# Turning residual columns and rotated heads by DMA instead of TensorE, loading weights five chunks ahead, and taking the heads' roots on GpSimd, in a two-layer hybrid encoder

## The chip, the cores and the metric

The kernel runs on one core of a Trainium2 chip. The metric is the device time of one execution in microseconds (us); the median of several runs is given. A core has TensorE (PE, with weight loads shown apart as PEld), VectorE (DVE), ScalarE (ACT), GpSimd (POOL) and SyncE (SP, which here issues transfers only). Each engine works through its own queue in order; engines wait for each other by semaphores.

## The reference, cut to what matters

The input is 256 tokens of width 2048, in float32. Two layers, each "norm, input projection, two kinds of attention with a SiLU gate, output projection, add", and a last norm.

```
def rms_norm(x, g):
    y = x * rsqrt(mean(x * x, axis=-1, keepdims=True) + EPS)
    return y * g

h = x
for layer in range(2):
    y = rms_norm(h, norm_g[layer])
    h = h + (even_layer(y, ...) if layer == 0 else odd_layer(y, ...))
return rms_norm(h, final_g)

# even: A = dilated attention (8 heads), B = neighbourhood attention (8 heads)
# odd:  C = windowed attention with a sink (8 heads, 2 for k and v)
#       D = dense attention (8 heads of q, 2 of k and v), q and k normed and rotated:
q = axial_rope(rms_norm(q, gq)); k = axial_rope(rms_norm(k, gk))
logits = einsum('bqhgd,bshd->bhgqs', q, k) * scale
p = softmax(logits); o = einsum('bhgqs,bshd->bqhgd', p, v)
# all: mix = concat of o * silu(gate); layer output = mix @ w_out
```

A head is 128 wide. What matters here are three places: the residual h behind the even layer must be turned (features onto partitions) to be the odd layer's input; each head of D needs one root per token for q and for k; the normed and rotated heads must be turned, too, before the logits.

## The kernel before, in words

**Numbers.** Every float32 factor is split in two, a rounded high part and the rest (`split`: ACT makes the high part, DVE subtracts). Products are sums of three matmuls, high by high, high by rest, rest by high (`mm3`, L102 to L104; `by_feature` does the same in two kinds of matmul, L267 and L271).

**Weights.** Every weight matrix is cut in chunks of 128 x 1024 (512 KB), in one list, `plan`, in the order of use. Class `Weights` (L55 on) loads a chunk to `wraw` (pool `wp`, 5 buffers, on SP, L65), ACT casts it to `whi` (L69) and DVE subtracts to `wlo` (L70), 3 buffers of each. `weights()` hands out the next chunk and prepares chunks so that two are ready beyond it (AHEAD = 2). One chunk is what TensorE works on between two calls of `step()`.

**Steps.** `step()` runs behind each chunk and lets three lists go on by a piece: `evac` (accumulators to SBUF), `post` (norm and rotation of D's heads, `normed_rope`, and the start of D's attentions) and `bg` (attentions, `attend`, written as generators). That sets where instructions are issued; the scheduler then sets the final order on each engine, and instructions marked with `keep_in_program_order` (the function `pinned` for transfers on SP) keep theirs.

**Stages.** Even layer: four groups of heads, each values by tokens (`ps_t`) and q, k, gates by features (`ps_f`), with the attentions of the group before alongside. Then the even output projection `project_out("even", next_input)`: four column blocks n of 512, eight chunks each; when block n is complete, `add_h` adds it to the residual `h[n]` and `next_input(n)` turns it: 8 transposes by TensorE to `ps_ht` (L660), split with the norm's gain into `xh`, `xl`. Then the odd layer: pass t = 0 by tokens (k and v of D), pass 1 (q pairs 0 and 1 of D), gates of pairs 0 and 1 by features, pass 2 (q pairs 2 and 3), gates 2 and 3, then branch C by features, the odd output projection and the end (`finish`, final norm and output).

**A head pair of D.** `heads_by_token` scales the accumulators into `rq` and sums squares into `dss` on ACT. `normed_rope` takes the root of four columns (`rsqrt`, on DVE: `rs_x` L159, `rs_y` L161, then three times `rs_t`, `rs_t`, `rs_z`, L165 to L168, the last into `drr`), multiplies `rq` by it (L351), rotates into `ru`, `rw` (L358, L362, L365), transposes `ru` by TensorE to `ps_tr` (L372) and splits into `qh`, `ql` (or `kh`, `kl`). There are five such sets: k and q0 to q3.

**Transposes by DMA that are there already.** In `attend` the probabilities are turned without TensorE: POOL copies the 16-bit halves of the words apart (`ph`, L463), two DMA transposes on SP turn them (`pa`, L87), POOL puts the halves together (`pt`, L474), then they are split (L482, L483).

**POOL** does those two copies, the bias tables of B (L403) and a copy of two sink values per head of C (L427).

Of the kernel before, what the change touches and what calls it, by code (L numbers as in the profile page):

```python
# [9 lines left out]
F32 = mybir.dt.float32  # L10
F32R = mybir.dt.float32r
BF16 = mybir.dt.bfloat16
I32 = mybir.dt.int32
# [5 lines left out]
P = 128  # L19
# [12 lines left out]
AHEAD = 2  # L32
RPB_R, RPB_C = 15, 31
# [3 lines left out]
def encoder(ctx, tc, a, out):  # L37
# [4 lines left out]
    wp = pool("wp", 5)  # L42
# [11 lines left out]
    class Weights:  # L54


        def __init__(self, src, hi=None, lo=None, x=None):
            raw = wp.tile([P, 1024], F32, tag="wraw", name="wraw")
            self.hi = hi or hp.tile([P, 1024], F32R, tag="whi", name="whi")
            self.lo = lo or hp.tile([P, 1024], F32R, tag="wlo", name="wlo")  # L60
            cuts = KK if x in (0, 1) else 1
            cols = [slice(i * 1024 // cuts, (i + 1) * 1024 // cuts) for i in range(cuts)]
            for i, c in enumerate(cols):
                load = nc.sync.dma_start if x is None else pinned
                load(raw[:, c], src[:, c])  # L65
                if x is not None and i == 0:
                    pinned(xraw[x], a["xt"][x].rearrange("p (k t) -> p k t", k=KK))
            for i, c in enumerate(cols):
                nc.scalar.copy(self.hi[:, c], raw[:, c])  # L69
                nc.vector.tensor_sub(self.lo[:, c], raw[:, c], self.hi[:, c].bitcast(F32))  # L70
                if x is not None:
                    for m in (i,) if cuts > 1 else range(KK):
                        k = x * KK + m
                        split(xh[k], xl[k], xraw[x][:, m, :], gcol[:, k : k + 1])

    plan, ready = [], []

    def weights(ahead=AHEAD):

        while plan and len(ready) <= ahead:  # L80
            src, x = plan.pop(0)
            ready.append(Weights(src, x=x))
        return ready.pop(0)
# [5 lines left out]
    def split(hi, lo, src, scale=None):  # L89

        if scale is None:
            nc.scalar.copy(hi, src)
            nc.vector.tensor_sub(lo, src, hi.bitcast(F32))
        else:
            nc.scalar.mul(hi, src, scale)  # L95
            nc.vector.scalar_tensor_tensor(
                out=lo, in0=src, scalar=scale, in1=hi.bitcast(F32), op0=ALU.mult, op1=ALU.subtract
            )
# [102 lines left out]


# [13 lines left out]
    def step():  # L216

        advance(evac)
        advance(post)
        attention()  # L220

# [14 lines left out]
    def drain():  # L236
        while evac or post or bg:
            step()

# [105 lines left out]
    def normed_rope(tag, q, ss, g, scale, give):  # L345

        rr = sm.tile([P, 4], F32, tag="drr", name="drr")
        rsqrt(rr, ss, 4, 1.0 / HD)
# [17 lines left out]
        yield  # L366
        yield
        yield from room(tag)
        tr = ps_at.tile([P, 2, S], F32, tag="at", name="ps_tr")
        for t in range(2):  # L370
            for hh in range(2):
                nc.tensor.transpose(tr[:, hh, t * P : (t + 1) * P], u[:, t, hh, :], ident)  # L372
        dst = pair(tag)
        split(*dst, tr, scale)
        give(dst)
        yield

# [28 lines left out]
    def attend(idx, q, kv, silu, frees, bias=None, sink=None, shared=False):  # L406
# [110 lines left out]
        nc.vector.tensor_mul(m, o, silu)  # L517
# [33 lines left out]
    def out_plan(kind):  # L551
        plan.extend((a["w_out_" + kind][n][pr], None) for n, pr in out_order(kind))
# [7 lines left out]
    for u in range(4):  # L560
        for pr, kind in even_order(u):
            if kind == "v":
                plan.extend((a["even_t"][u][j], None if u else j) for j in range(8))
            else:
                plan.extend((a["even_f"][2 * u + pr]["qkg".index(kind)][j], None) for j in range(4))
    out_plan("even")
    for t, fs in ((0, ()), (1, (10, 11)), (2, (12, 13))):
        plan.extend((a["odd_t"][t][j], None) for j in range(8))
        plan.extend((a["odd_f"][f][j], None) for f in fs for j in range(4))
    plan.extend((a["odd_f"][f][j], None) for f in (0, 1, 2, 6, 3, 7, 4, 8, 5, 9) for j in range(4))  # L570
# [82 lines left out]

    def next_input(n):

        for c in range(2):
# [17 lines left out]

    project_out("even", next_input)
# [22 lines left out]
    def evict_heads(st, which, acc):  # L698

        for i, key in enumerate(which):  # L700
            if key is not None:
# [3 lines left out]
                post.append(normed_rope("k" if key == "k" else "q", q, ss, g, scale, give))  # L705
            yield

    def when_ready(i, st, s):
        attend_odd(1, i, st, s)
        yield  # L710

    def evict_odd(branch, kind, i, acc, st):
# [6 lines left out]
        else:  # L719
            s = gate(acc, rhalf)  # L720
            if branch:
                post.append(when_ready(i, st, s))
            else:
                attend_odd(branch, i, st, s)
# [21 lines left out]
    def beside(n, i):  # L746
# [5 lines left out]
        if n == 2 and i % 2:  # L752
            j = i // 2
            room = X[j].rearrange("p k c t -> p (k c t)")
            final.append(Weights(a["w_out_odd"][NN - 1][late[j]], room[:, :1024], room[:, 1024:]))
# [42 lines left out]
    def finish(n, t, r, cols=full, scalar=False):  # L798
# [7 lines left out]
        queue = nc.scalar if scalar and t else nc.sync  # L806
        pin(queue.dma_start(out[t * P : (t + 1) * P, n * 512 + cols.start : n * 512 + cols.stop], y))
# [17 lines left out]
    finish(0, 1, r, halves[0])  # L825
    finish(1, 1, r, scalar=True)
    finish(0, 1, r, halves[1])
    finish(2, 1, r, scalar=True)
    finish(3, 1, r, halves[0])
    finish(3, 1, r, halves[1])  # L830
# [85 lines left out]
```

## Time and profile before

| what | value |
|---|---|
| time, median of 3 runs | 820.77 us (820.68 to 821.61) |
| profiled execution | 820.54 us, of which span 818.8 us |
| granted TensorE clock, mean | 0.996 |
| PE busy | 808.6 us, 99% of the span, 4317 instructions |
| DVE busy | 576.1 us, 70%, 856 instructions |
| ACT busy | 447.3 us, 55%, 712 instructions |
| POOL busy | 110.6 us, 14%, 88 instructions |
| HBM read | 155.64 MB; 194 GB/s over the span |

The profile is of one execution. A row of the timeline gives start, duration, engine, line, operation, output<-input, shape and count. A row of groups gives count, busy time and mean duration of one in ns, then the idle time of the engine just before and what ended most of it. A row of windows gives the window and for each engine the busy us and, in brackets, the instructions: PE, PEld, DVE, ACT, POOL, then the granted clock, the DMA share and GB/s. A matmul's duration is longer than the distance to the next one because they are pipelined: the distance of starts is what it costs.

### The profile page before, as it was taken

Reading aid. Unit: us, or ns where it says so; the run is one execution under the profiler, and the core shown is the slowest. Engines: PE = TensorE matmul, PEld = TensorE weight load, DVE = VectorE, ACT = ScalarE, POOL = GpSimd, SP = SyncE. Lnnn points to the kernel's source line nnn. Section 1 sums busy time; section 2 is a strip of 40 time slices with the busy share of each in tenths; the row PEclk is TensorE's granted clock in tenths of the full one; section 3 lists DMA queues with packets and bytes.
Section 4 is the critical chain, followed back from the end, with each engine's and each line's share of the span. In section 5 each row is a group of like instructions: output and inputs, shape, how many; then the busy total and the mean of one; then the engine's idle time right before and its main releaser. Section 6 shows DMA issues by size and latency. Waiting matters only on the chain.

```text
span 818.8 us, 11775 instructions
## 1 busy us (share of the span) xinstructions
PE 808.6 (99%) x4317; PEld 695.1 (85%) x4317; DVE 576.1 (70%) x856; ACT 447.3 (55%) x712; POOL 110.6 (14%) x88
## 2 busy tenths in 40 slices
PE   9999999999999999999999999999999999999995
PEld 7888888888888888888888888888899888888884
DVE  6677675677857886587655577685987777775763
ACT  7745454554545554455445544657666665664651
POOL 0002020021302140050200000002112222221000
PEclk9999999999999999999999999999999999999998
DMA  8956765575755766565654555556577775777532
GB/s 336 354 210 209 271 213 177 208 213 168 233 182 171 241 173 220 203 194 197 213 177 172 186 186 172 200 192 198 161 183 226 224 222 184 227 197 225 209 126 104
DMA packets 90682, 166.91 MB, mean 204 GB/s; under 512 B 48960, under 2 KB 50112, under 8 KB 90560
## 3 DMA queue, kind: packets, MB, share of 16 engines
q1 hardware_dynamic: 90192, 165.61, 62.5%
q8 instruction: 34, 0.56, 0.3%
q10 hardware_dynamic: 432, 0.54, 0.2%
q14 instruction: 24, 0.20, 0.1%
HBM read 155.64 MB, written 3.05 MB: 194 GB/s over the span
## 4 chain that ended last, share of the span: by engine, by line
PE 98%; DMA 0%; ACT 0%; DVE 0%; issue 0%; ACTq 0%; DVEq 0%
PE ps_f L267 34%; PE ps_f L271 17%; PE ps_t L102 14%; PE ps_t L103 14%; PE ps_t L104 14%; PE ps_s L103 1%; PE ps_s L104 1%; PE ps_s L102 1%; PE ps_out L103 1%; PE ps_out L102 1%; PE ps_out L104 1%; PE ps_ht L660 0%; DMA wraw<-in_even_t 0%; PE ps_tr L372 0%; ACT h L803 0%; ACT whi L69 0%
## 5 line engine op out<-in xcount | busy, mean ns | idle before, releaser
L70 DVE TENSOR_TENSOR wlo<-wraw,whi 128x1024 fp32r<-128x1024 f32 (+1 forms) x270 | 344.4, 1276 | 187.8 <-ACT whi L69 187.3
L69 ACT CAST whi<-wraw 128x1024 fp32r<-128x1024 f32 (+1 forms) x270 | 281.9, 1044 | 300.9 <-PE ps_t L104 130.7
L267 PE MATMUL ps_f<-x,whi 128*128 128x512 f32 x1184 | 372.3, 396 | 0.0
L271 PEld LDWEIGHTS ps_f<-x,wlo 128*128 128x128 f32 x1184 | 222.4, 188 | 52.9 <-DVE wlo L70 0.7
L271 PE MATMUL ps_f<-x,wlo 128*128 128x256 f32 x1184 | 233.0, 278 | 0.0
L267 PEld LDWEIGHTS ps_f<-x,whi 128*128 128x128 f32 x1184 | 180.9, 189 | 0.5
L102 PE MATMUL ps_t<-whi,x 128*128 128x512 f32 (+1 forms) x256 | 96.8, 381 | 0.3 <-ACT x L95 0.3
L103 PE MATMUL ps_t<-wlo,x 128*128 128x512 f32 (+1 forms) x256 | 96.4, 379 | 0.0
L104 PE MATMUL ps_t<-whi,x 128*128 128x512 f32 (+1 forms) x256 | 96.1, 377 | 0.0
L463 POOL COPY ph<-pr 128x1024 uint16<-128x1024 uint16 x32 | 39.5, 1233 | 418.1 <-ACT pr L453 252.0
L102 PE MATMUL ps_t<-whi,mh 128*128 128x512 f32 x240 | 93.8, 391 | 0.0
L103 PE MATMUL ps_t<-wlo,mh 128*128 128x512 f32 x240 | 93.7, 391 | 0.0
L104 PE MATMUL ps_t<-whi,ml 128*128 128x512 f32 x240 | 93.6, 390 | 0.0
L104 PEld LDWEIGHTS ps_t<-whi,x 128*128 128x128 f32 x256 | 48.5, 189 | 9.0
L102 PEld LDWEIGHTS ps_t<-whi,x 128*128 128x128 f32 x256 | 48.5, 189 | 9.0 <-ACT x L95 0.6
L474 POOL COPY pt<-pa 128x1024 uint16<-128x1024 uint16 x32 | 50.4, 1576 | 37.5 <-DMA pa<-ph 37.2
L103 PEld LDWEIGHTS ps_t<-wlo,x 128*128 128x128 f32 x256 | 48.6, 190 | 8.2
L104 PEld LDWEIGHTS ps_t<-whi,ml 128*128 128x128 f32 x240 | 45.1, 188 | 9.3
L103 PEld LDWEIGHTS ps_t<-wlo,mh 128*128 128x128 f32 x240 | 45.1, 188 | 8.9
L102 PEld LDWEIGHTS ps_t<-whi,mh 128*128 128x128 f32 x240 | 45.1, 188 | 8.9
L445 ACT ACTIVATE pr<-lg,mn 128x256 f32<-128x256 f32 (+1 forms) x48 | 24.0, 501 | 16.5 <-POOL ph L463 8.9
L403 POOL TENSOR_TENSOR bias<-maskB,rpb 128x512 f32<-128x512 f32 x8 | 12.5, 1567 | 138.5 <-DMA rpb<-rows 138.5
(129 smaller groups left out, 664.4 us busy)
## 6 DMA issues: line engine op xcount, KB each, us to landing
wraw<-in_even_f SPq DMA_DIRECT2D x96, 512.0 KB, 3.5
wraw<-in_odd_f SPq DMA_DIRECT2D x56, 512.0 KB, 3.7
wraw<-in_w_out_even SPq DMA_DIRECT2D x32, 512.0 KB, 3.3
wraw<-in_w_out_odd SPq DMA_DIRECT2D x32, 512.0 KB, 4.3
wraw<-in_even_t SPq DMA_DIRECT2D x30, 512.0 KB, 4.3
wraw<-in_odd_t SPq DMA_DIRECT2D x24, 512.0 KB, 3.2
xraw<-in_xt SPq DMA_DIRECT2D x8, 256.0 KB, 7.0
h<-in_x SPq DMA_DIRECT2D x4, 512.0 KB, 8.6
```

The source lines that it names most:

```text
L69: nc.scalar.copy(self.hi[:, c], raw[:, c])
L70: nc.vector.tensor_sub(self.lo[:, c], raw[:, c], self.hi[:, c].bitcast(F32))
L102: nc.tensor.matmul(dst, lh, rh, start=first, stop=False, skip_group_check=True)
L103: nc.tensor.matmul(dst, lh, rl, start=False, stop=False, skip_group_check=True)
L104: nc.tensor.matmul(dst, ll, rh, start=False, stop=last, skip_group_check=True)
L267: nc.tensor.matmul(acc[:, f, :], w.hi[:, c], xx[k], start=k == 0, stop=False, skip_group_check=True)
L271: nc.tensor.matmul(acc[:, f, :S], w.lo[:, c], xh[k], start=False, stop=k == KC - 1, skip_group_check=True)
L403: nc.gpsimd.tensor_tensor(b, maskB.unsqueeze(1).to_broadcast([P, 2, S]), raw, op=ALU.subtract)
L445: nc.scalar.activation(p[:, t, :W], lg[:, t, :W], AF.Exp, bias=mn[:, t : t + 1], scale=-1.0, accum_out=den[:, t : t + 1],)
L463: nc.gpsimd.tensor_copy(halves, words)
L474: nc.gpsimd.tensor_copy(words.bitcast(U16).rearrange("p c (q s) -> p s c q", s=2), st[i])
```

## The change

It has five parts.

1. *Residual.* For n = 0, 1, 2 the eight TensorE transposes of `next_input` are replaced by `turned_input`, two per n: POOL copies 256 columns' halves apart (`hh`), two pinned DMA transposes on SP (`ha`), POOL joins (`hw`), ACT and DVE split. They are advanced by `turning()` in `step()`. For n = 3 TensorE still transposes.
2. *Heads.* In `normed_rope` the four TensorE transposes per set are replaced in the same way (`rh`, L414 of the changed kernel; `ra`; `rt`, L424). The attention of a pair is started at the end of `normed_rope` (`begin`), not behind its gate.
3. *Roots.* The five roots of D's heads are taken by `rsqrt4` on POOL, 14 instructions each in place of 11 on DVE (in each of the three rounds, three DVE instructions become four).
4. *Weights.* Loading and preparing are separated. From the even output projection on (`lead`), loads are pinned on SP and five chunks not yet prepared are kept loaded. The four late chunks of the odd output projection, which are prepared into the free input tiles X, come by way of the plan.
5. *The end.* All output transfers are issued by SP; the second half of the last block goes out as one piece of 512, not two of 256.

In instructions: PE 4319 to 4275, DVE 858 to 802, POOL 93 to 185, SP 419 to 442, ACT 609 to 607.

```diff
-    def weights(ahead=AHEAD):
-        while plan and len(ready) <= ahead:
-            src, x = plan.pop(0)
-            ready.append(Weights(src, x=x))
+    def load_ahead():
+        while plan and len(loaded) < (lead or [1])[0]:
+            loaded.append(Weights(*plan.pop(0)))
+
+    def weights():
+        while (plan or loaded) and len(ready) <= AHEAD:
+            load_ahead()
+            ready.append(loaded.pop(0))
+            ready[-1].prepare()
+        if lead:
+            load_ahead()
         return ready.pop(0)
...
+                load = pinned if lead or x is not None else nc.sync.dma_start
...
+    def rsqrt4(dst, ss, mean):
+        new = lambda name, dt=F32: sm.tile([P, 4], dt, tag=name, name=name)
+        x, y = new("rs_x"), new("rs_y", I32)
+        nc.gpsimd.tensor_scalar(x, ss, mean, EPS, ALU.mult, ALU.add)
+        nc.gpsimd.tensor_scalar(y, x.bitcast(I32), -0.5, 1597463007.0, ALU.mult, ALU.add)
+        y = y.bitcast(F32)
+        for it in range(3):
+            t, z = new("rs_t"), dst if it == 2 else new("rs_z")
+            nc.gpsimd.tensor_mul(t, y, y)
+            nc.gpsimd.tensor_mul(t, t, x)
+            nc.gpsimd.tensor_scalar(t, t, -0.5, 1.5, ALU.mult, ALU.add)
+            nc.gpsimd.tensor_mul(z, t, y)
+            y = z
...
     def step():
         advance(evac)
         advance(post)
         attention()
+        turning()
...
         rr = sm.tile([P, 4], F32, tag="drr", name="drr")
-        rsqrt(rr, ss, 4, 1.0 / HD)
+        rsqrt4(rr, ss, 1.0 / HD)
...
         nc.vector.tensor_add(u, u, w)
         yield
+        halves = tp.tile([P, 2, 2, S], U16, tag="tmp2", name="rh")
+        across = tp.tile([P, 2, 2, S], U16, tag="tmp2", name="ra")
+        nc.gpsimd.tensor_copy(halves, u.rearrange(...).bitcast(U16).rearrange("p t (k s) -> p t s k", s=2))
+        yield
+        for t in range(2):
+            pinned(across[:, :, :, t * P : (t + 1) * P]..., halves[:, t]..., transpose=True)
+        yield
+        yield
+        words = tp.tile([P, 2, S], F32, tag="rpb", name="rt", bufs=1)
+        nc.gpsimd.tensor_copy(words.bitcast(U16).rearrange("p c (q s) -> p s c q", s=2), across)
+        yield
         yield from room(tag)
-        tr = ps_at.tile([P, 2, S], F32, tag="at", name="ps_tr")
-        for t in range(2):
-            for hh in range(2):
-                nc.tensor.transpose(tr[:, hh, t * P : (t + 1) * P], u[:, t, hh, :], ident)
         dst = pair(tag)
-        split(*dst, tr, scale)
+        split(*dst, words, scale, tc.keep_in_program_order)
         give(dst)
         yield
+        begin()
...
     def next_input(n):
+        if n < NN - 1:
+            for c in range(2):
+                turns.append(turned_input(n, c))
+                steps[id(turns[-1])] = 0
+            square_sums(parts1, n)
+            return
...
+    lead.append(RAW)
     project_out("even", next_input)
...
-        queue = nc.scalar if scalar and t else nc.sync
-        pin(queue.dma_start(out[...], y))
+        pin(nc.sync.dma_start(out[...], y))
...
-    finish(3, 1, r, halves[0])
-    finish(3, 1, r, halves[1])
+    finish(3, 1, r)
```

`turned_input(n, c)` has the same steps as the piece in `normed_rope`, on columns of `h[n]`, with tiles `hh`, `ha`, `hw`.

What the order of instructions shows, on three engines.

DVE, where pass 1's first head pair (q0) is normed. Before, the end of its root and the rotation, with the next root (q1) begun:

```order
L166 SCALAR_TENSOR_TENSOR rs_t<-rs_t,rs_x 128x4
L70 TENSOR_TENSOR wlo<-wraw,whi 128x1024
L168 SCALAR_TENSOR_TENSOR drr<-rs_t,rs_z 128x4
L159 TENSOR_SCALAR rs_x<-dss 128x4
L351 SCALAR_TENSOR_TENSOR rq<-rq,drr,gq 128x128 x4
L358 TENSOR_TENSOR ru<-rq,cosT 128x256
L362 TENSOR_TENSOR rw<-rq,sinT 128x4x32 x2
L358 TENSOR_TENSOR ru<-rq,cosT 128x256
L362 TENSOR_TENSOR rw<-rq,sinT 128x4x32 x2
L70 TENSOR_TENSOR wlo<-wraw,whi 128x1024
L365 TENSOR_TENSOR ru<-ru,rw 128x512
L161 TENSOR_SCALAR rs_y<-rs_x 128x4
```

After, from the splits of weights ahead of the first `rq`:

```order
L76 TENSOR_TENSOR wlo<-wraw,whi 128x1024 x2
L396 SCALAR_TENSOR_TENSOR rq<-rq,drr,gq 128x128 x4
L403 TENSOR_TENSOR ru<-rq,cosT 128x256
L407 TENSOR_TENSOR rw<-rq,sinT 128x4x32 x2
L76 TENSOR_TENSOR wlo<-wraw,whi 128x1024
L403 TENSOR_TENSOR ru<-rq,cosT 128x256
L407 TENSOR_TENSOR rw<-rq,sinT 128x4x32 x2
L76 TENSOR_TENSOR wlo<-wraw,whi 128x1024
L410 TENSOR_TENSOR ru<-ru,rw 128x512
L396 SCALAR_TENSOR_TENSOR rq<-rq,drr,gq 128x128 x2
L76 TENSOR_TENSOR wlo<-wraw,whi 128x1024
L356 TENSOR_TENSOR qf<-ps_f,qf 128x512
```

The root's rows are gone from DVE; the splits of weights (L76) stand between and behind the steps that take `drr`.

POOL, the stretch of the odd layer with D's heads. Before, it had nothing there but the attentions' copies:

```order
L463 COPY ph<-pr 128x1024 x2
L474 COPY pt<-pa 128x2x512 x2
L463 COPY ph<-pr 128x1024 x2
L474 COPY pt<-pa 128x2x512 x2
L463 COPY ph<-pr 128x1024 x2
L474 COPY pt<-pa 128x2x512 x2
```

After, the end of the second of the two roots of pass 1 (that of q1, behind that of q0) and what follows it:

```order
L227 TENSOR_TENSOR rs_z<-rs_t,rs_z 128x4
L224 TENSOR_TENSOR rs_t<-rs_z 128x4
L225 TENSOR_TENSOR rs_t<-rs_t,rs_x 128x4
L226 TENSOR_SCALAR rs_t<-rs_t 128x4
L227 TENSOR_TENSOR drr<-rs_t,rs_z 128x4
L414 COPY rh<-ru 128x1024
L424 COPY rt<-ra 128x2x512
L414 COPY rh<-ru 128x1024
L518 COPY ph<-pr 128x1024 x2
L529 COPY pt<-pa 128x2x512
L424 COPY rt<-ra 128x2x512
L529 COPY pt<-pa 128x2x512
```

Both roots, 28 instructions in a row, stand ahead of the first copy of the rotated heads, and those copies mix with the attentions' own.

TensorE, at the first logits of D (`ps_s`; `x_87` is the tile of the first four of sixteen blocks of features in pass 2, `x_88` that of the next four). Before:

```order
L102 MATMUL ps_t<-whi,x_88 128x512
L103 MATMUL ps_t<-wlo,x_88 128x512
L104 MATMUL ps_t<-whi,x_88 128x512
L102 MATMUL ps_s<-kh,qh 128x256
L103 MATMUL ps_s<-kl,qh 128x256
L104 MATMUL ps_s<-kh,ql 128x256
```

After:

```order
L115 MATMUL ps_t<-whi,x_87 128x512
L116 MATMUL ps_t<-wlo,x_87 128x512
L117 MATMUL ps_t<-whi,x_87 128x512
L115 MATMUL ps_s<-kh,qh 128x256
L116 MATMUL ps_s<-kl,qh 128x256
L117 MATMUL ps_s<-kh,ql 128x256
```

The first logits stand within the first two chunks of pass 2 now, and within the next two before.

108 lines of the change are left out of this document (76 added, 32 removed).

## The prediction

> **What bounds the kernel now.** I read the page first: busy times, the chain, the groups. Then came the matmuls one by one at the transposes that go, and the stretches in which VectorE (DVE) is fullest.
>
> ```profile
> span 818.8 us, 11775 instructions
> ...
> PE 808.6 (99%) x4317; PEld 695.1 (85%) x4317; DVE 576.1 (70%) x856; ACT 447.3 (55%) x712; POOL 110.6 (14%) x88
> ...
> PE 98%; DMA 0%; ACT 0%; DVE 0%; issue 0%; ACTq 0%; DVEq 0%
> ...
> L102 PE MATMUL ps_t<-whi,x 128*128 128x512 f32 (+1 forms) x256 | 96.8, 381 | 0.3 <-ACT x L95 0.3
> ```
>
> TensorE is busy for 808.6 of 818.8 us and is 98% of the chain that ended last; the one wait of it inside the kernel is 0.3 us for ACT. So time goes only where TensorE gets less to do, and comes only where something makes it wait. The profiled execution took 820.54 us, 1.7 around its span, and lies 0.23 below the median of 820.77. About 0.2% (1.6 us) is what a measurement here tells from no change: faster is below 819.1, slower above 822.4.
>
> **What TensorE loses.** The residual columns n=0..2 (24 of 32 `ps_ht` transposes) and all 20 `ps_tr` transposes go. They run between matmuls that start 0.2275 us apart, so their price is what they add to the starts. One set of each in the trace:
>
> ```profile
> 426.09 0.39 PE L102 MATMUL ps_t<-whi,mh 128*128 128x512 f32 x1
> 426.36 0.44 PE L660 MATMUL ps_ht<-ident,h 128*128 128x128 f32 x2
> 426.55 0.49 PE L103 MATMUL ps_t<-wlo,mh 128*128 128x512 f32 x1
> 426.88 0.40 PE L104 MATMUL ps_t<-whi,ml 128*128 128x512 f32 x1
> 427.12 0.82 PE L660 MATMUL ps_ht<-ident,h 128*128 128x128 f32 x6
> 427.69 0.48 PE L102 MATMUL ps_t<-whi,mh 128*128 128x512 f32 x1
> ...
> 428.47 0.39 PE L102 MATMUL ps_t<-whi,mh 128*128 128x512 f32 x1
> ```
>
> ```profile
> 510.30 0.39 PE L103 MATMUL ps_t<-wlo,x 128*128 128x512 f32 x1
> ...
> 511.21 0.39 PE L104 MATMUL ps_t<-whi,x 128*128 128x512 f32 x1
> 511.44 0.60 PE L372 MATMUL ps_tr<-ident,ru 128*128 128x128 f32 x4
> 511.79 0.48 PE L102 MATMUL ps_t<-whi,x 128*128 128x512 f32 x1
> ...
> 512.34 0.40 PE L104 MATMUL ps_t<-whi,x 128*128 128x512 f32 x1
> ```
>
> The plain distance of two matmuls is read from 510.30 to 511.21, four steps in 0.91: 0.2275. From 426.09 to 428.47 are six steps (two of their rows are left out): 2.38 us against 1.37, so this set costs 1.01; three sets, 3.05. From 511.21 to 512.34 are three steps (512.11 left out): 1.13 against 0.68, 0.45; five sets, 2.25. Saved in all: 5.3 us. This is the sure term, because nothing else on TensorE changes but the order.
>
> One chunk of TensorE's work, the unit below:
>
> ```profile
> 520.08 0.61 PE L267 MATMUL ps_f<-x,whi 128*128 128x512 f32 x2
> ...
> 522.86 0.40 PE L267 MATMUL ps_f<-x,whi 128*128 128x512 f32 x1
> ```
>
> A chunk of weights by features takes 2.78 (16 matmuls lie between these two starts); one by tokens is 12 matmuls, 2.73.
>
> **Loads five chunks ahead: nothing.** SP's loads already wait for a free buffer and not for the program:
>
> ```profile
> SPq L65 <- DVE wlo L70: 443.9, 201, 5.8
> ```
>
> ```profile
> 556.41 2.51 SPq L87 DMA_TRANSPOSE pa<-ph  x2
> ```
>
> ```profile
> wraw<-in_odd_f SPq DMA_DIRECT2D x56, 512.0 KB, 3.7
> ```
>
> The first row is SP's waits (us in total, times, longest): 201 loads wait for the split that frees their buffer. The pool has five buffers before and after, so a load cannot leave earlier than it did. Its 3.7 us to landing are covered by the five buffers, 5 x 2.78 = 14 us of matmuls. What the pins change: the 22 added transposes, 1.25 us of SP each (556.41: two in 2.51), now stand in line with the loads, and where a transpose waits for POOL's copy the loads behind it wait too. A wait of 3 us there fits into the 14; without that cover it would cost its 2.5 to 3.7 us at each of 11 places. Taken at zero.
>
> **Residual by DMA: nothing on the path.** POOL copies `hh` (a copy of that size: 1.04 below), two transposes issue (2.5) and land (I take as much again), POOL copies `hw` (1.4 to 1.9), ACT and DVE split: some 9 to 10 us. The n=2 columns are the last that go this way; eight chunks of n=3, 8 x 2.73 = 21.8 us of TensorE's work, stand between them and the odd projection. If that cover were gone, 10 us.
>
> ```profile
> 420.00:480.00 60.00, 60.00 (x280) 49.12 (x279) 36.12 (x44) 32.32 (x51) 0.00 (x0) 1.00 0.53 184
> 495.00:521.00 26.00, 26.00 (x119) 21.54 (x118) 17.00 (x34) 13.30 (x23) 0.00 (x0) 1.00 0.56 184
> 521.00:545.00 24.00, 24.00 (x138) 20.93 (x137) 21.70 (x57) 14.74 (x33) 0.00 (x0) 1.00 0.54 185
> 566.00:600.00 34.00, 34.00 (x200) 29.66 (x199) 30.92 (x69) 21.61 (x50) 5.75 (x4) 1.00 0.62 175
> ```
>
> In these rows (PE, PEld, DVE, ACT, POOL busy) DVE has 24 of 60 us and POOL all of them free in the output projection; it is in the last two that DVE is nearly full, and there lie the D heads.
>
> **The roots on POOL.** Five roots leave DVE (55 instructions) and become 14 dependent ones each on POOL. Beside them the trace has:
>
> ```profile
> 525.12 0.16 DVE L159 TENSOR_SCALAR rs_x<-dss 128x4 f32<-128x4 f32 x1
> ...
> 527.01 1.23 DVE L70 TENSOR_TENSOR wlo<-wraw,whi 128x1024 fp32r<-128x1024 f32 x1
> 528.15 0.16 DVE L168 SCALAR_TENSOR_TENSOR drr<-rs_t,rs_z 128x4 f32<-128x4 f32 x1
> ...
> 528.35 1.14 DVE L351 SCALAR_TENSOR_TENSOR rq<-rq,drr,gq 128x128 f32<-128x128 f32 x4
> 529.41 0.42 DVE L358 TENSOR_TENSOR ru<-rq,cosT 128x256 f32<-128x256 f32 x1
> ```
>
> ```profile
> 0.24 0.10 POOL L906 MEMSET const-float32-0.0<- 128x1 f32 x1 [0.24 <-issue]
> ...
> 1.10 0.29 POOL masks.py:199 TENSOR_SCALAR_AFFINE_SELECT ident<-ident 128x128 f32<-128x128 f32 x1
> ```
>
> ```profile
> 649.61 1.72 POOL L427 COPY lg<-nsink 128x2 f32<-128x2 f32 x2 [5.61 <-DVE ptl L483]
> ```
>
> ```profile
> 554.79 0.49 ACT L453 ACTIVATE pr<-pr,rden 128x256 f32<-128x256 f32 x1
> ```
>
> ```profile
> 555.35 1.04 POOL L463 COPY ph<-pr 128x1024 uint16<-128x1024 uint16 x1 [156.65 <-ACT pr L453]
> ```
>
> ```profile
> 592.20 1.38 POOL L474 COPY pt<-pa 128x1024 uint16<-128x1024 uint16 x1 [0.25 <-POOL ph L463]
> ```
>
> DVE's root took 3.2 us with one split inside, 0.2 per instruction. No row shows a 128x4 operation on POOL. From below: the 0.10 of a memset and hardly a gap, 0.17, so 14 x 0.17 = 2.4 us a root, less than DVE's. From above: the tiny copy L427, 0.86 each, 12 us a root. That row stands beside a split of DVE, and I put most of it down to that. Between: the select over 128 elements took 0.29, some 0.19 of it fixed (128 elements cost 0.10 more in it than one does in the memset); what lies between two dependent steps is 0.07 where POOL takes over from ACT (554.79 + 0.49 to 555.35) and 0.25 in the row of 592.20, behind POOL itself. With 0.07: 0.26 an instruction, 3.7 us a root; with 0.25: 0.44, 6.2 us. I take 0.26, nearest to the select.
>
> The Trainium skill, GPSIMD Engine Reference, "Elementwise — side-by-side cycle accounting", has a two-input add on GpSimd 1.96 times as long as on VectorE and keeps to VectorE for elementwise work. By that rule the root would take 1.96 x 0.2 x 14 = 5.5 us, an estimate, near the upper end here; no row here shows it for 128x4.
>
> **What waits for a root.** DVE works in order. Its first `rq` (L396 after) waits for `drr`, and behind it stand the splits of weights that TensorE eats, one per 2.78 us, two chunks in hand. Zone 1 is the gates of the first two pairs: accumulators full at T, `dss` at most 5.0 later (520.08 to 525.12), `drr` 3.7 after that. From the first `rq` to the split `ql` of pair 0 DVE's list has, in the changed order, 8 `rq` (2.3), two `ru`, `rw` sets and adds (4.1), 6 weights' splits (6.8) and four 512-wide steps (2.4): 15.6. So `ql` at T + 24.3 bare. The first logits now stand behind eight gate chunks and one token chunk, T + 25.1 (before: four token chunks). Slack 0.8.
>
> Into that slack fall the POOL copies that are new, since POOL and DVE hold each other up:
>
> ```profile
> 586.70 1.65 POOL L463 COPY ph<-pr 128x1024 uint16<-128x1024 uint16 x1 [21.19 <-ACT pr L453]
> ```
>
> ```profile
> 585.54 0.69 DVE L331 SCALAR_TENSOR_TENSOR silu<-ge,qf 128x512 f32<-128x512 f32 x1
> ...
> 587.34 1.02 DVE L165 TENSOR_TENSOR rs_t<-rs_z 128x4 f32<-128x4 f32 x1
> ```
>
> From 585.54 on come three 512-wide steps in 1.80, the 0.6 each of the list above. Then a step of 0.16 on DVE took 1.02 beside the copy, which itself took 1.65 in place of 1.04. The Trainium skill, SBUF — State Buffer, "SBUF: two separate sides", calls the port that DVE (with two SBUF inputs) and GpSimd share an exclusive lock for the whole instruction; these two rows and the 1.72 above agree. So each copy may cost DVE 0.8 to 1.1. Zone 1 has `rh` and `rt` of pair 0, and some of pair 1's: 0.7 to 2.6. Stall 0 to 1.8; I take 0.3, since about half of such meetings are paid by POOL.
>
> Zone 2 (pairs 2 and 3, behind the next pass by tokens, with a T of its own): `dss` 5.0, root 3.7, DVE's list 17.2, because steps of the first pairs' attention are in it, copies (`rh`, `rt`, `ph`, `pt`) 2 to 6.4: T + 27.9 to 32.3. The logits of pair 2 stand behind nine chunks and 18 matmuls of the attention (2.8): T + 27.9. Stall 0 to 4.4; I take 1.7, in the lower half for the same reason. The root of k lies where DVE has 9 of 26 us free: 0.
>
> **The end.** ACT issues no transfer any more, SP all; h3 goes out as one. ACT's issue of 0.37 goes, SP's line gets longer by one: -0.2 to +0.2, taken 0.
>
> Sum: 820.54 - 5.3 + 0.3 + 1.7 = 817.2, with the 0.23 to the median 817.5.
>
> **Rivals.**
> - Full saving: the copies fall where DVE is idle, or roots run at 0.17 and end 1.3 us sooner in each zone. For it: DVE loses 55 instructions (55 x 0.2 = 11 us of its queue); against it: 21.70 of 24 busy. 820.8 - 5.3 = 815.5.
> - Saving eaten: 0.33 an instruction, 4.6 us a root (0.9 more in both zones and about 1 at k), copies at the middle of their bounds: 1.7 + 2.9 + 0.7 = 5.3. Time 820.8, no change. A change that doesn't do what it says ends here too, as the loads do already.
> - The other side, one mechanism: a root at the 0.44 end, 2.5 us later each. DVE stands at L396, the splits behind it come late, and the pair 1 root, queued on POOL behind that of pair 0, holds DVE a second time (0.7). Stalls: zone 1 0.3 + 2.5 + 0.7, zone 2 1.7 + 2.5, k 1: 8.7, time 824.2. It decides from 6.9 us of stalls, about 0.39 an instruction. For it: the gap of 0.25 and the DVE meetings; against it: the 1.10 row. At the far end (0.86, 12 us a root) each zone would lose another 5.8 and the second root as much again: 840 and more. The 1.96 of the Trainium skill's page, quoted above, puts the root just at this rival's threshold, at some 822.4 by estimate.
>
> **How the numbers follow.** Likeliest, part given back, 817.5: 0.37. Full saving 815.5: 0.25. Eaten, 820.8: 0.20. Slow root, 824: 0.18. So faster 0.62, same 0.20, slower 0.18. The range runs from 814.9 (the full saving, with half a microsecond for the end and the transposes' price) to 823.0, which leaves out the upper part of the slow root. The likeliest alone: 816.3 to 819.1.
>
> **What would show it.** TensorE's matmuls about 5.3 us shorter, no `ps_tr`, eight `ps_ht`. `rs_x` to `drr` on POOL 3 to 4.5 us. Waits of TensorE on `wlo` or `ql` of some 2 us in all, near the first logits of pairs 0 and 2; none at the odd projection's start. `ps_s` waits above 6 us, or DVE's L396 waiting more than 5 us for POOL at several places, would make me wrong upwards; no waits at all, downwards.

## The result, and the profile after

The changed kernel takes 832.29 us (median of 4 runs, 831.78 to 833.00) against 821.19 beside it: ratio 1.0135, interval 1.0119 to 1.0151. It is 11.1 us slower, where 817.5 with a range of 814.9 to 823.0 was forecast. The profiled execution took 832.62 us with a span of 830.8, 12.0 more than before.

The page of the changed kernel, the same lines as before (span, busy times, chain):

```profile
span 830.8 us, 11769 instructions
...
PE 807.1 (97%) x4273; PEld 690.6 (83%) x4273; DVE 583.4 (70%) x800; ACT 448.2 (54%) x712; POOL 165.0 (20%) x180
...
PE 83%; DMA 4%; POOL 4%; DVE 4%; issue 2%; ACT 2%; SPq 1%; ACTq 0%; DVEq 0%; POOLq 0%
```

TensorE's share of the chain falls from 98% to 83%; POOL, DVE and DMA, which had none, have 4% each. TensorE's waits in the changed kernel (engine, line, releaser, then us in total, times, longest):

```profile
PE ps_f L316 <- DVE wlo L76: 9.4, 6, 2.6
PE ps_s L117 <- DVE ql L109: 3.0, 2, 1.6
PE ps_idle L138 <- DVE idle L135: 1.2, 1, 1.2
PE ps_t L115 <- ACT x L108: 1.1, 2, 0.6
PE ps_t L116 <- DVE wlo L76: 1.0, 2, 0.7
```

Both kernels have the 1.2 us of `ps_idle`, at the very start. Besides it there were 0.3 us of waits before, and now there are 14.5: 10.4 for splits of weights, 3.0 for the low half of a head, 1.1 for the input. Of these 14.5, 1.6 lie in the first 31 us, ahead of everything that the change aims at. DVE's own waits show what it stood for:

```profile
DVE rq L396 <- POOL drr L227: 12.9, 5, 3.7
...
DVE ru L403 <- DMA ra<-rh: 3.7, 2, 2.5
```

All five roots made DVE wait, up to 3.7 us each. Zone 1 in detail, first DVE's timeline, then POOL's:

```profile
524.18 1.22 DVE L76 TENSOR_TENSOR wlo<-wraw,whi 128x1024 fp32r<-128x1024 f32 x1 [1.39 <-ACT whi L75]
529.13 1.14 DVE L396 SCALAR_TENSOR_TENSOR rq<-rq,drr,gq 128x128 f32<-128x128 f32 x4 [3.72 <-POOL drr L227]
...
530.92 1.22 DVE L76 TENSOR_TENSOR wlo<-wraw,whi 128x1024 fp32r<-128x1024 f32 x1
...
532.80 1.22 DVE L76 TENSOR_TENSOR wlo<-wraw,whi 128x1024 fp32r<-128x1024 f32 x1
533.94 0.69 DVE L410 TENSOR_TENSOR ru<-ru,rw 128x512 f32<-128x512 f32 x1
537.51 1.35 DVE L396 SCALAR_TENSOR_TENSOR rq<-rq,drr,gq 128x128 f32<-128x128 f32 x2 [2.89 <-POOL drr L227]
538.78 1.21 DVE L76 TENSOR_TENSOR wlo<-wraw,whi 128x1024 fp32r<-128x1024 f32 x1
```

```profile
525.20 0.27 POOL L219 TENSOR_SCALAR rs_x<-dss 128x4 f32<-128x4 f32 x1 [5.26 <-ACT junk L387]
...
528.89 0.20 POOL L227 TENSOR_TENSOR drr<-rs_t,rs_z 128x4 f32<-128x4 f32 x1
529.18 0.35 POOL L219 TENSOR_SCALAR rs_x<-dss 128x4 f32<-128x4 f32 x1
529.62 0.19 POOL L220 TENSOR_SCALAR rs_y<-rs_x 128x4 int32<-128x4 int32 x1
529.89 0.20 POOL L224 TENSOR_TENSOR rs_t<-rs_y 128x4 f32<-128x4 f32 x1
530.17 4.52 POOL L225 TENSOR_TENSOR rs_t<-rs_t,rs_x 128x4 f32<-128x4 f32 x1
...
537.28 0.20 POOL L227 TENSOR_TENSOR drr<-rs_t,rs_z 128x4 f32<-128x4 f32 x1
```

Three things are to be seen. From 524.18 to 530.92 DVE starts no split, 6.7 us, while TensorE eats one chunk per 2.78. The undisturbed root (525.20 to 529.09) takes 3.9 us, 0.28 an instruction, nearly what was forecast. But the next root, q1's, takes 8.3 (529.18 to 537.48): one step of it, 0.20 elsewhere, lasts 4.52, from the start of DVE's run of rotation steps and splits (530.19) to its end at 534.63. Then DVE waits for that root in turn (2.89), again with a split behind it. DVE itself is not slowed in that run: its splits take 1.22 as elsewhere.

TensorE pays a second time right behind. Windows of the changed kernel (us, busy us of PE, PEld, DVE, ACT, POOL, then the granted clock):

```profile
530.00:541.00 11.00, 7.52 (x43) 5.93 (x42) 8.11 (x17) 2.59 (x3) 7.55 (x13) 1.00 0.28 96
541.00:544.20 3.20, 3.20 (x13) 2.71 (x12) 2.46 (x4) 2.16 (x3) 0.00 (x0) 0.50 1.02 247
```

After a stretch in which it was busy 7.5 of 11 us, the clock granted is half for 3.2 us, which is 1.6 us lost.

Where the 12.0 us lie is seen from the starts of four matmuls: the first of the even output projection, the first of the odd layer, the first of the odd output projection, and the last of all. Before, then after:

```profile
381.63 0.40 PE L102 MATMUL ps_t<-whi,mh 128*128 128x512 f32 x1
474.76 0.39 PE L102 MATMUL ps_t<-whi,x 128*128 128x512 f32 x1
718.63 0.40 PE L102 MATMUL ps_t<-whi,mh 128*128 128x512 f32 x1
809.85 0.28 PE L104 MATMUL ps_e<-x,ml 128*128 128x256 f32 x1
```

```profile
383.04 0.40 PE L115 MATMUL ps_t<-whi,mh 128*128 128x512 f32 x1
473.07 0.39 PE L115 MATMUL ps_t<-whi,x 128*128 128x512 f32 x1
731.38 0.40 PE L115 MATMUL ps_t<-whi,mh 128*128 128x512 f32 x1
822.60 0.28 PE L117 MATMUL ps_e<-x,ml 128*128 128x256 f32 x1
```

The even layer takes 1.4 us more, behind the waits of the first 31 us. The even output projection takes 90.0 in place of 93.1: the residual's saving, 3.1, is there. The odd layer takes 258.3 in place of 243.9, 14.4 more. The odd output projection takes the same 91.2, and from the last matmul to the span's end are 8.2 in place of 9.0. In the odd layer the gaps between starts of TensorE's matmuls come to 14.3 (listed further below) and the half clock to 1.6; less the 2.25 of the heads' transposes that is 13.7 of the 14.4. The rest, 0.8, I have not split up.

SyncE's queue in zone 2:

```profile
579.75 13.30 SPq L100 DMA_DIRECT2D wraw<-in_odd_f  x3
593.14 2.50 SPq L100 DMA_TRANSPOSE pa<-ph  x2
595.73 0.54 SPq L100 DMA_DIRECT2D wraw<-in_odd_f  x1
596.32 2.52 SPq L100 DMA_TRANSPOSE ra<-rh  x2
```

```profile
590.11 1.04 POOL L414 COPY rh<-ru 128x1024 uint16<-128x1024 uint16 x1
```

`rh` was ready at 591.15; its transposes left at 596.32, behind two loads and two transposes of the attention. The loads waited for a buffer: from 575 to 598 SP's waits for DVE's `wlo` are 18.0 us in four places.

### The profile page after: what moved, and what is told of

The parts are those of the page before. It is cut to its first block, busy times and chain, and to the rows that moved or that the text cites. A ratio compares the mean times of both kernels' runs of the same rounds, so it can differ in the third digit from the quotient of the medians.

```text
span 830.8 us, 11769 instructions
## 1 busy us (share of the span) xinstructions
PE 807.1 (97%) x4273; PEld 690.6 (83%) x4273; DVE 583.4 (70%) x800; ACT 448.2 (54%) x712; POOL 165.0 (20%) x180
## 3 DMA queue, kind: packets, MB, share of 16 engines
HBM read 155.64 MB, written 3.05 MB: 191 GB/s over the span
## 4 chain that ended last, share of the span: by engine, by line
PE 83%; DMA 4%; POOL 4%; DVE 4%; issue 2%; ACT 2%; SPq 1%; ACTq 0%; DVEq 0%; POOLq 0%
PE ps_f L312 29%; PE ps_f L316 15%; PE ps_t L115 11%; PE ps_t L117 11%; PE ps_t L116 11%; DVE wlo L76 2%; DMA ra<-rh 1%; DMA wraw<-in_even_f 1%; ACT whi L75 1%; SPq L100 1%; DMA wraw<-in_even_t 1%; POOL rs_t L225 1%; PE ps_s L117 1%; PE ps_out L116 1%; PE ps_out L115 1%
## 5 line engine op out<-in xcount | busy, mean ns | idle before, releaser
L76 DVE TENSOR_TENSOR wlo<-wraw,whi 128x1024 fp32r<-128x1024 f32 (+1 forms) x270 | 349.9, 1297 | 174.9 <-ACT whi L75 173.5
L529 POOL COPY pt<-pa 128x1024 uint16<-128x1024 uint16 x32 | 56.9, 1778 | 27.7 <-DMA pa<-ph 27.5
L116 PEld LDWEIGHTS ps_t<-wlo,x 128*128 128x128 f32 x256 | 48.2, 188 | 10.4 <-DVE wlo L76 2.2
L458 POOL TENSOR_TENSOR bias<-maskB,rpb 128x512 f32<-128x512 f32 x8 | 12.4, 1552 | 137.5 <-DMA rpb<-rows 137.5
L537 ACT CAST pth<-pt 128x512 fp32r<-128x512 f32 x32 | 19.8, 618 | 23.3 <-POOL pt L529 23.1
```

Source lines behind the costliest of these rows:

```text
L116: nc.tensor.matmul(dst, lh, rl, start=False, stop=False, skip_group_check=True)
L458: nc.gpsimd.tensor_tensor(b, maskB.unsqueeze(1).to_broadcast([P, 2, S]), raw, op=ALU.subtract)
L529: nc.gpsimd.tensor_copy(words.bitcast(U16).rearrange("p c (q s) -> p s c q", s=2), st[i])
L537: tc.keep_in_program_order(nc.scalar.copy(hi, st[i]))
```

## The experiments

Theory A: DVE, in order, stands at a root's first use, and the splits of weights behind it come late. Rivals: B, the turned heads' buffers; C, transposes behind pinned loads on SP; D, small POOL instructions and DVE holding each other up. All times are medians, ratios are to the kernel before, run on the same chip (its median 820.8 to 821.5). Kernels measured on different chips are compared by their ratios.

**Roots back on DVE.**

```diff
-        rsqrt4(rr, ss, 1.0 / HD)
+        rsqrt(rr, ss, 4, 1.0 / HD)
```

> The changed kernel with one part undone: the five roots of D's heads are on VectorE again (11 instructions each), all else as changed. Theory A (VectorE stands at the first multiplication by drr until GpSimd's root is done, and the weights' splits stand behind it): the waits of VectorE for drr (12.9 us in five places) go, and with them TensorE's stalls at 507 (1.1 us), 530 (1.7), 537 (2.2, and 1.2 more at half the granted clock right behind it) and 586 to 593 (3.2): 832.3 - 9.4 = about 823. Theory B (the turning of the heads is the slow path: a pair's rotation waits for a buffer that the pair before holds until its transposes have been issued): TensorE's stalls only move to the rotation, 829 to 832. 'Loads' theory C (transposes stand on SyncE behind pinned loads that wait for buffers): also 829 to 832.

820.63 us, ratio 0.9994 (0.9985 to 1.0004): 11.7 us off the changed kernel, more than the 9.4 that theory A gave; B and C fall as main causes. But of the 5.3 us that TensorE was to save, nothing is left over. TensorE's waits:

```profile
PE ps_f L316 <- DVE wlo L76: 4.4, 2, 3.9
```

The stall of 3.9 is new, from 589 on. DVE and POOL there:

```profile
591.07 2.29 DVE L76 TENSOR_TENSOR wlo<-wraw,whi 128x1024 fp32r<-128x1024 f32 x1
```

```profile
590.99 1.34 POOL L529 COPY pt<-pa 128x1024 uint16<-128x1024 uint16 x1 [0.85 <-DMA pa<-ph]
```

A split of 1.2 takes 2.29 beside a POOL copy. Just before, from 586.12 to 590.11, three root steps on DVE (0.16 alone) take 1.00, 1.20 and 1.24 beside copies of POOL. Together that is some 4 us by which this split is late, as much as TensorE stands (3.86). The half clock follows here too: the granted clock is 0.64 from 593.4 to 597.4, some 1.4 us lost.

**Without the lead.**

```diff
-    lead.append(RAW)
```

> The changed kernel without the five-chunk lead: loads are neither pinned nor issued ahead of the chunk's preparing, as before; all else as changed. Theory C (SyncE's line: a transpose that could leave waits behind pinned loads that wait for a buffer, 1.9 us at 538.5 and 5.2 us at 591): the stalls at 547 to 552 (2.0 us) and at 601 and 606 (4.5) go, 832.3 - 6.5 = about 826. Theory A (root): nothing changes on VectorE's wait for drr, 831 to 833. Theory B (buffers): 831 to 833.

828.32 us, 1.0084 (1.0067 to 1.0101): 4.0 us off, between what theories A and C gave. C is a part, and only a part: DVE's wait for `drr` stays, 14.4 us.

**Other buffers for rh and ra.**

```diff
-        halves = tp.tile([P, 2, 2, S], U16, tag="tmp2", name="rh")
-        across = tp.tile([P, 2, 2, S], U16, tag="tmp2", name="ra")
+        halves = pp.tile([P, 2, 2, S], U16, tag="bias", name="rh", bufs=4)
+        across = pp.tile([P, 2, 2, S], U16, tag="bias", name="ra", bufs=4)
```

> The changed kernel with other buffers for the rotated heads' two copies (rh, ra): they take the four buffers of the bias tables, idle in this stage, in place of the two that ru and rw use; all else as changed. Theory B (buffers): VectorE's waits of ru for the transposes (3.7 us in two places) go, and with them the stalls of TensorE at 547 (0.4) and 601 (2.8): about 829. Theory C: ql still comes late from SyncE's line, so 831 to 833. Theory A: 831 to 833.

832.58 us, 1.0132 (1.0114 to 1.0150). No change; B falls. DVE's wait of `ru` for `ra<-rh` is gone from its list, and the time has not followed it.

**Heads by TensorE again, roots still on POOL.** The copies and DMA transposes of `normed_rope` are replaced by the four TensorE transposes of before.

> The changed kernel with the rotated heads turned by TensorE as before (20 transposes, 5 x 0.45 = 2.25 us), roots still on GpSimd, residual by DMA, five chunks ahead. Theory A alone: the root's stalls (9.4 us) stay and those of the DMA path (6.5) go: 832.3 + 2.25 - 6.5 = about 828. Theories B and C, if the DMA path had caused all of it: 832.3 + 2.25 - 16 = about 818.5.

832.87 us, 1.0141 (1.0126 to 1.0156). Slower than the 828 of theory A alone, so the time that was put down to the DMA path did not come off with it. All of the loss is still there, and that path is not what the roots need to do harm.

**Of D's heads only the roots changed.** Heads and residual by TensorE, no lead.

```diff
-        if n < NN - 1:
+        if False:
...
-    lead.append(RAW)
```

> The changed kernel with the residual and the rotated heads turned by TensorE and without the lead, as before: of the parts that touch D's heads only the roots on GpSimd are left (with the earlier start of D's attentions and the new end). Theory A (the root's latency with VectorE standing at its first use): 832.9 of the kernel with heads by TensorE, plus 3.05 for the residual's transposes, less some 4 for the lead = about 832, at least 828. Rival (the roots cost only because GpSimd and SyncE have the other new copies and transposes to do): 821 to 823.

837.77 us, 1.0200 (1.0186 to 1.0214): the roots on POOL, together with the earlier start (some 4 us alone, below), cost 16 us. That is 6 above the likeliest value of theory A; the granted clock is below 0.6 here behind three waits, which end at 545, 593 and 603. POOL has no other work in the gates of the first pairs. The waits of DVE, and POOL's step in zone 2:

```profile
DVE rq L396 <- POOL drr L227: 16.3, 5, 3.7
```

```profile
590.53 6.26 POOL L224 TENSOR_TENSOR rs_t<-rs_y 128x4 f32<-128x4 f32 x1
```

```profile
594.91 0.68 DVE L529 TENSOR_TENSOR ptl<-pt,pth 128x512 fp32r<-128x512 f32 x1
595.52 1.21 DVE L76 TENSOR_TENSOR wlo<-wraw,whi 128x1024 fp32r<-128x1024 f32 x1
596.65 0.68 DVE L356 TENSOR_TENSOR qf<-ps_f,qf 128x512 f32<-128x512 f32 x1
```

The step ends at 596.79, just behind the first DVE instruction of the run that has an input in PSUM (`ps_f`, at 596.65); all those from 590.56 on read both inputs from SBUF. So in these two places a 0.2 us step stood through nine and eleven DVE instructions, until DVE was idle or read PSUM. It is not so beside every run of DVE: beside the four `rq` at 529.13 in the changed kernel, which read both inputs from SBUF too, three steps took 0.35, 0.19 and 0.20. What decides it, these runs do not tell.

**A root nobody reads.** On the fastest kernel (below, 817.50) the roots run on DVE and a second time on POOL.

```diff
+        spare = sm.tile([P, 4], F32, tag="spare", name="spare")
+        rsqrt4(spare, ss, 1.0 / HD)
         rsqrt(rr, ss, 4, 1.0 / HD)
```

> The fastest kernel so far (817.5: residual by DMA, lead, roots on VectorE, heads by TensorE, attentions started behind their gates) with the five roots taken a second time on GpSimd, 70 small instructions whose result nobody reads. Theory A (the cost is VectorE standing at a root's first use, in order, with the splits behind it): nobody waits, so no cost, 817.5 to 818.5. Rival D (GpSimd's small instructions and VectorE hold each other up): the same meetings as in the changed kernel, 822 or more.

818.10 us, 0.9966 (0.9954 to 0.9979), against 0.9959 (0.9946 to 0.9971) without it: no cost that shows. Its POOL steps are held up as well, though none for longer than 1.28:

```profile
528.33 1.06 POOL L224 TENSOR_TENSOR grs_t<-grs_y 128x4 f32<-128x4 f32 x1
...
530.08 1.11 POOL L226 TENSOR_SCALAR grs_t<-grs_t 128x4 f32<-128x4 f32 x1
```

but nobody waits, and TensorE has no wait for `wlo` or `ql`. So D, as a cost by itself, falls for meetings of this length; in the 4.5 us one of the changed kernel it was POOL that stood, and DVE ran on. The harm is done by DVE waiting for the root. What D does is make that root late (8.3 in place of 3.9), and how much of the loss goes back to that was not measured by itself.

**A later first use.** Two steps between the root on POOL and L396, so that the splits of two more chunks may go ahead of it.

```diff
         rsqrt4(rr, ss, 1.0 / HD)
+        yield
+        yield
```

> The changed kernel with two more steps between the root and its first use (two yields behind rsqrt4), so that several weights' splits stand ahead of the multiplications by drr on VectorE; the roots stay on GpSimd and the heads on DMA. Theory A (the cost is VectorE standing at drr with splits behind it): TensorE's 9.4 us of stalls at 507, 530, 537 and 586 to 593 go, some of it comes back as later logits, 821 to 826. Rival D (the cost is GpSimd's instructions and VectorE's holding each other up, as the 4.5 us of one GpSimd step at 530 show): just as many meetings, 829 to 833.

> The changed kernel with two more steps between the root on GpSimd and its first use, and rq in the bias tables' buffers (in the earlier kernel of this kind rq is written over before its last reader; its time of 824.9 alone is read). Theory A: as there, 823 to 826, since splits of weights stand ahead of the multiplications. If the earlier time came from the reused buffers: 829 to 833.

824.93 us, 1.0038 (1.0025 to 1.0050), and with other buffers 825.05, 1.0059 (1.0045 to 1.0073): 6 to 8 us off the changed kernel with the roots still on POOL, as theory A gave. The waits say why:

```profile
PE ps_f L316 <- DVE wlo L76: 1.8, 2, 1.1
...
PE ps_t L116 <- DVE wlo L76: 1.2, 2, 0.7
```

```profile
DVE rq L398 <- POOL drr L227: 12.4, 4, 4.0
```

DVE stands at `drr` almost as long as before (12.4, after 12.9), but TensorE's waits for splits fall from 10.4 to 3.0. It is what stands behind the wait that costs. In both of these kernels, and in the three with the later start and heads by DMA below, part of the result comes out of other data than the reference's. Which tile does it was not settled; `rq`, which two expectations name, is not it, since buffers of its own moved neither the outcome nor the time. The instructions on TensorE, DVE and POOL are the same in kind and number, so their times are read.

**The residual by DMA.** Roots on DVE, heads by TensorE.

> The changed kernel with two parts undone: roots on VectorE and rotated heads turned by TensorE, as before. What is left is the residual by DMA, the five-chunk lead, the earlier start of D's attentions and the new end. The prediction's term for the residual (24 transposes less, 3.05 us, nothing on the path): 821.2 - 3.05 = about 818.1. If the lead or the earlier start costs something (loads pinned ahead of the transposes of the attentions): 819.5 to 822.

822.01 us, 1.0008 (0.9999 to 1.0017): no gain. But TensorE waits for the heads at the first logits, which stand earlier in its order:

```profile
PE ps_s L117 <- DVE ql L109: 2.2, 2, 2.0
...
PE ps_s L115 <- ACT qh L108: 0.9, 1, 0.9
```

So the start behind the gates was put back, with and without the lead:

```diff
-                st["s", i] = s
+                post.append(when_ready(i, st, s))
...
-        begin()
```

> Only the residual by DMA and the new end are left of the change: roots on VectorE, heads turned by TensorE, no lead, and D's attentions started behind their gates as before. The kernel with the residual, the lead and the earlier start measured 822.0, with TensorE waiting 3.1 us for ql and qh at the early logits. If the residual's term (3.05 us) is right and the earlier start is what took it back: 821.4 - 3.05 = about 818. If the residual's path by DMA costs what it saves: 821 to 822.

> As the last one, but with the five-chunk lead and its pinned loads. It tells the lead from the earlier start. If the earlier start took the residual's gain back: about 818, as without the lead. If the lead did: 821 to 822.

818.18 us, 0.9959 (0.9947 to 0.9972), and with the lead 817.50 us, 0.9959 (0.9946 to 0.9971). The residual's saving is there, 0.41% or 3.4 us, with the new end in it, and the lead neither gives nor takes anything that shows. The earlier start alone, between 822.01 and 817.50, costs about 4 us (4.0 by the ratios, 4.5 by the medians). The 817.50 kernel beats both: residual by DMA, everything of D's heads as before. Its waits of TensorE, both in the first 10 us and none at the odd layer's start:

```profile
PE ps_t L115 <- ACT x L108: 1.1, 2, 0.6
```

**Heads by DMA with roots on DVE.** Without the residual by DMA:

> The changed kernel with roots on VectorE and the residual turned by TensorE: of the large parts the heads by DMA and the lead are left. If the stall of 4 us at 589 in the kernel with roots on VectorE belongs to the heads' copies on GpSimd beside VectorE: 820.6 + 3.05 = about 823.7. If it belongs to the residual's copies or their transposes: 821.2 - 2.25 = about 819.

824.61 us, 1.0040 (1.0028 to 1.0053), about 4 more than with the residual by DMA (820.63): the residual's part adds up, and the stall, 3.8 us here, belongs to the heads. With residual, and the later start:

> Residual and heads by DMA, roots on VectorE, no lead, D's attentions started behind their gates. With the later start the heads' longer way (copies and transposes) has several chunks more: the full saving of 5.3 us, about 816. Rival (GpSimd's copies hold VectorE in the gates of pairs 2 and 3, as in the kernel with roots on VectorE, where one split took 2.3 us and TensorE stood 3.9): 820 to 821.

> Residual and heads by DMA, roots on VectorE, no lead, attentions started behind their gates, and the scaled heads rq in the four buffers of the bias tables, so that a late multiplication finds them (with the shared buffers of the earlier kernel of this kind, rq is written over before its last reader; only that kernel's time is read). 822.7 was measured there. If the copies on GpSimd beside VectorE are the cost: 821 to 823. If buffers were: about 816.

822.72 us, 1.0021 (1.0012 to 1.0030), and 822.73 with `rq` elsewhere, 1.0027 (1.0015 to 1.0038). The full saving doesn't come, with later logits either. POOL's copies alone, on the fastest kernel:

```diff
         nc.vector.tensor_add(u, u, w)
         yield
+        halves = pp.tile([P, 2, 2, S], U16, tag="bias", name="rh", bufs=4)
+        nc.gpsimd.tensor_copy(halves, u...)
+        words = pp.tile([P, 2, S], F32, tag="bias", name="rt", bufs=4)
+        nc.gpsimd.tensor_copy(words..., halves...)
```

> The same fastest kernel with the heads' two GpSimd copies of 128 x 1024 added per pair (ten in all, the first from ru, the second from the first) without a reader and without the DMA transposes between them; heads are still turned by TensorE. If copies beside VectorE's full stretches are what took back the gain in the kernels with heads by DMA and roots on VectorE (a split of 2.3 us, TensorE standing 3.9): 820 to 822. If it is the way's length (transposes, SyncE's line, splits behind late data): 817.5 to 818.5.

819.80 us, 0.9987 (0.9979 to 0.9996) against 0.9959 (0.9946 to 0.9971): ten copies without a reader cost about 2.3 us, a little below what was expected and as much as the heads' 20 transposes on TensorE (2.25). The kernels with heads by DMA and the later start lie 7 us above the full saving (822.7 against 817.8, the mean of the two without heads by DMA, less 2.25); the copies account for 2.3 of it. The rest, the transposes in SP's line and the later splits, was not taken apart.

**The later start on the changed kernel.**

> The changed kernel with one part undone: D's attentions start behind their gates as before; roots on GpSimd, heads and residual by DMA, lead on. Theory A (splits of weights queue on VectorE behind a root on GpSimd): that does not depend on when the logits come; the waits on wlo (10.4 us and the half clock behind them) stay and those on ql (3.0 us) go: 827 to 830. Rival (the earlier start is what makes the roots late for something): 818 to 823.

833.48 us, 1.0146 (1.0131 to 1.0162). Above the 827 to 830 of theory A, and far from the rival's. With the roots on POOL the waits on `wlo` only grow:

```profile
PE ps_t L116 <- DVE wlo L76: 7.0, 5, 2.0
PE ps_f L316 <- DVE wlo L76: 5.2, 5, 2.0
```

## Why the prediction was wrong, point by point

- *TensorE loses 5.3 us.* Right as far as it shows. The residual's share, forecast 3.05, is 3.1 in the even output projection, and the path by DMA is covered, as said. The heads' share, 2.25, never comes out as time. It is read only by subtraction: with the roots back on DVE the odd layer takes 2.9 more than before, with a gap of 4.0 and some 1.4 of half clock in it, so 2.5 less without them.
- *A root takes 3.7 us on POOL.* Right for an undisturbed one: 3.9, 0.28 an instruction. The choice nearest to the select's row came out, but with bounds from 0.17 to 0.86 the closeness is partly luck.
- *What waits for a root.* **This is the step that failed.** The slack was worked out for one dependent, `ql`, by adding up DVE's list from the first `rq` on. The splits of weights, named in the same paragraph as "two chunks in hand", were counted there as DVE's time, but when each of them was due at TensorE was not worked out. Behind a wait of 3.7 us and two rotation steps, DVE starts no split for 6.7 us against a chunk of 2.78, and TensorE waits. Forecast for zone 1 was 0.3 us; TensorE's gaps there, in the starts of its matmuls, are 1.7 at 530, 2.2 at 538, 0.4 at 547 and 1.5 at 550. In zone 2, forecast 1.7, they are 0.7, 2.5, 2.8 and 1.6; of these the 2.8 stands behind DVE's wait for a turned head (`ra`, 2.5), not for a root. The root of k, put at nothing because DVE had 9 of 26 us free, made DVE wait 3.3 us and cost a gap of 0.9 at 507: free time elsewhere does not help a split that stands behind a wait. And `ql` itself came later than its sum: 24.3 us after the accumulators were full by forecast, 32.9 in the trace (518.94 to 551.83). The sum left out the way of the heads through POOL and SP, priced at 9 to 10 us for the residual; from the end of the rotation to the start of `ql` it took 15.7 (534.63 to 550.31), in which `rh` stood behind the second root on POOL until 537.42. The experiment with heads by TensorE shows that this way is not needed for the loss. (A slip beside these: eight gate chunks and one token chunk are 25.0, not 25.1, so the slack was 0.7.)
- *Meetings of POOL and DVE cost 0.8 to 1.1 each.* That price came from a copy, which runs as soon as DVE lets it in once. A chain of small steps meets DVE's full queue with each step, and one of them stood for 4.5 us (6.3 in the kernel with the roots alone). The rival with the slow root had the mechanism, "holds DVE a second time", with 0.7 us for it and a threshold of 0.39 an instruction. It came about at 0.28, since the second root's 8.3 us were not those of its instructions. So the direction was among the rivals, and its chance of 0.18 was too low for the same reason.
- *Loads five chunks ahead: nothing.* Right by themselves (817.50 with, 818.18 without). In the changed kernel they cost 4.0 us: the forecast looked at loads behind waiting transposes and left out transposes behind waiting loads.
- *The earlier logits.* They were treated as a due time with 0.8 us of slack, not as a cost. By itself, the earlier start takes about 4 us.
- *Half clock behind long waits* was not thought of: 1.6 us in the changed kernel.
- *The end:* taken 0. From the last matmul's start to the span's end are 9.0 us in the trace of before and 8.1 to 8.7 in those of all kernels with the new end, so it gains 0.3 to 0.9. It was not tried alone, and before has a single trace.

The Trainium skill, SBUF — State Buffer, "SBUF: two separate sides", has DVE with two SBUF inputs and a GpSimd instruction exclude each other for a whole instruction. The step that ended when DVE read PSUM (596.65 and 596.79) agrees with its condition. The three steps that went through at once beside `rq` (529.18 to 530.09) do not. The rule as quoted would price one meeting at one instruction, too; these runs show a small step kept out through nine and eleven of DVE's in a row.

## What to carry to other kernels

Before work is moved to an engine that is idle, ask what stands behind its first use in the queue of the engine that waits, and put each of those through the sum of due times, not only the result of the chain. Here a root off VectorE saved it 2.2 us of work (11 steps of 0.2) and cost it up to 3.7 us of standing, a loss because VectorE feeds the engine that bounds; where nobody waited for it, the same root cost nothing that shows. And when a change has several parts, the one that gains (here the residual, 0.4%) is found by undoing the others one at a time.

## What the runs showed of the hardware that I had not expected

- A 128x4 step on GpSimd takes 0.20 us and 0.28 from start to start. Met by a run of VectorE instructions with both inputs in SBUF it took 4.52 and 6.26 in two places, 1.06 to 1.28 in others, and beside `rq` hardly longer than alone (0.35, 0.19, 0.20).
- The granted clock falls to 0.50 behind short waits: gaps of 1.7 us and, 7 us later, 2.2 us (the windows above), for about 3 us. Behind the wait of 2.5 us in zone 2 of the same kernel there was none, nor behind that of 2.8 (1.00 from 604 to 607), so the length of one wait does not decide it; what does, these runs don't tell. The window behind that wait, granted clock 1.00:

```profile
593.00:596.00 3.00, 3.00 (x19) 2.64 (x19) 3.00 (x7) 0.52 (x2) 0.00 (x0) 1.00 0.81 212
```

The Trainium skill, TensorE: Matmul & The Clock Gate, "Part 1: The HAM clock gate (the "warmup" mystery)", gives half rate after about 3.4 us of idling; in the changed kernel no single wait was that long (2.8 us at most), so by that rule there would have been no half clock.
